# Choosing expert rows by float32 picks and an indexed fetch, and returning every pass's result through TensorE

## The chip, the core and the metric

The kernel runs on one core of one Trainium2 chip. The metric is device microseconds of one execution. The core has TensorE (PE; its weight loads are PEld), VectorE (DVE), ScalarE (ACT), GpSimd (POOL), a sync engine (SP) whose queue issues most transfers, and 16 DMA engines. [...]

## What is computed

One decoder layer on 512 tokens of width 1024: a mixer of mLSTM and sliding-window heads, a layer norm, a mixture of 32 experts, a second layer norm.

```python
x = layer_norm(ALPHA * x + hybrid_mixer(x, ...), ln1_w, ln1_b)
g_idx = argmax(x @ w_group_router + b_group_router)          # 4 groups
e_in = (x @ w_expert_router + b_expert_router)[8 experts of g_idx]
top_v, top_i = top_k(e_in, 2)
combine = one_hot(8 * g_idx + top_i) * softmax(top_v) * group_probability
for e in range(32):                                          # D_EXPERT = 256
    h = silu(x @ w_exp_gate[e]) * (x @ w_exp_up[e])
    out += combine[:, e] * (h @ w_exp_down[e])
x = layer_norm(ALPHA * x + out, ln2_w, ln2_b)
```

All tensors are float32. The weights of one expert are 3 MB.

## The kernel before

**Mixer.** Float32 products are made of a high and a low part in fp32r, three products each. The projection's weights come in eleven column groups; the first in three loads (`load_w`, `split_w`, `unit_att`). Small tables come on the GpSimd queue, among them the convolution's weights: `cw` in four transfers of 1,024 single float32 elements, `cb` in one.

**Router stage.** Tokens stand in four groups `c` of 128. For each the output projection (`out_mm`, `ml_late`) is summed in PSUM, then `norm_a` (statistics) and `norm_b` (application) give `x1[c]`; `route_t` transposes it, `route_m` multiplies by the router's weights, `route_d` finds two experts a token, `route_r` the rank of a token in its expert, `first_hot` the one-hot matrix of places. `NB` says for each half which engines apply the norm: V is two operations on DVE, the others go over ACT and POOL. `x1_hi` (ACT) and `x1_lo` (POOL) split `x1` into two fp32r parts. The order of PE, DVE, ACT and POOL is written out by hand in this stage.

**Expert passes.** Thirteen passes hold 128 places each, kinds `BBBCABABABBCC` (B: two experts, A: two, C: four). The first three passes have the experts 0 to 5 (their weights are fetched ahead); the others have experts by load, whose numbers `eid` come from `slots_a` and `slots_e`. A pass multiplies its rows `xs` by gate and up (`gu_part`), makes `h` (`pair_h`, `dn_t`) and multiplies by down (`dn_mm`). Rows come for two passes at a time: `first_pick` for passes 0 and 1, `pairs_x` for 2 to 11: 64 fp32r products of 128x256 with the one-hot of places (`pick`, L1014). Only pass 12 fetches rows of `x1` from DRAM (`xd`) by index, `fetch`, and transposes them. The results of passes 0 to 7 (`KEPT = 8`) are scaled and stored in DRAM (`y_store`, table `yd`); at passes 8 and 9 each token fetches its two rows (`y_fetch`, `y_add`). Passes 8 to 11 are added by TensorE: `add_back`, for each 128 tokens and half width two products of 128x512 (L1185) with the one-hot `back_hot` and one DVE addition.

**Transfers.** Expert weights come over SP's queue in pieces of 1 MB (a gate and an up piece of 512 KB each, or a down piece) into 16 ring slots (`ring0` 7, `ring1` 5, `ring2` 4) and two borrowed ones. A slot is loaded again after the products that read it (`release`, `prefetch`).

Of the kernel before, what the change touches and what calls it, by code (L numbers as in the profile page):

```python
# [80 lines left out]
def layer_kernel(ctx, tc, x, w_in, conv_w, conv_b, gate_bias, norm_w, sinks, w_out, ln1_w, ln1_b,  # L81
# [504 lines left out]

    def load_part(ts, e, i, js=None):
# [137 lines left out]
    x1, x1h, x1l, amh, mlm, pys = [], [], [], {}, {}, {}  # L725
# [151 lines left out]
    def norm_b(c, h):  # L877
        xc_ = x1[c]
        mv = n1[c][1]
        hs = slice(h * 512, (h + 1) * 512)  # L880
        xh_ = xc_[:, hs]
        if NB[c][h] == "V":
            V.scalar_tensor_tensor(xh_, xh_, mv[:, 0:1], l1w[:, hs], op0=OP.subtract, op1=OP.mult)
            V.scalar_tensor_tensor(xh_, xh_, mv[:, 2:3], l1b[:, hs], op0=OP.mult, op1=OP.add)
        else:
            if h == 0 or NB[c][0] == "V":
                G.tensor_scalar(mv[:, 3:4], mv[:, 2:3], mv[:, 0:1], -1.0, op0=OP.mult, op1=OP.mult)
            A.activation(xh_, xh_, AF.Identity, bias=mv[:, 3:4], scale=mv[:, 2:3])
            (V if NB[c][h] == "M" else G).tensor_mul(xh_, xh_, l1w[:, hs])
            G.tensor_add(xh_, xh_, l1b[:, hs])  # L890

    def x1_parts(c, halves):
        v = x1[c].rearrange("p (q j) -> p j q", j=8)
        if len(x1h) == c:
            for t, n in ((x1h, "x1h"), (x1l, "x1l")):
                t.append(slot(n, F32R)[:, :DM].rearrange("p (j q) -> p j q", j=8))
        for q in [slice(0, P)] if halves is None else [slice(64 * h, 64 * h + 64) for h in halves]:
            yield x1h[c][:, :, q], x1l[c][:, :, q], v[:, :, q]

    def x1_hi(c, halves=None):  # L900
        for hi, _, v in x1_parts(c, halves):
            A.activation(hi, v, AF.Copy)

    def x1_lo(c, halves=None, eng=G):
        for hi, lo, v in x1_parts(c, halves):
            eng.tensor_tensor(lo, v, hi, op=OP.subtract)
# [95 lines left out]
    def hot_tiles():  # L1002
        return slot("ohr", F32R)[:, :DM].rearrange("p (c s) -> p c s", c=NCH)

    def hot(o, c, col, n=2 * P):
        d, k = o[:, c, 0:n], iot[:, 0:n]
        V.tensor_scalar(d, k, col[:, 0:1], None, op0=OP.is_equal)
        yield
        V.scalar_tensor_tensor(d, k, col[:, 1:2], d.bitcast(F32), op0=OP.is_equal, op1=OP.add)
        yield  # L1010

    def pick(p_, j2, o, c, g, n=2):
        for s, w in enumerate((x1h, x1l)):
            TE.matmul(p_[:, j2, 0:P * n], w[c][:, 2 * g + j2], o[:, c, 0:P * n], start=c == 0 and s == 0 and j2 == 0,  # L1014
                      stop=c == NCH - 1 and s == 1 and j2 == 1)

    def pick_out(xs, p_, g, n=2, eng=None):
        d = xs[g // 2][:, 2 * (g % 2):2 * (g % 2) + 2, 0:P * n]
        if g % 2 and eng is None:
            V.tensor_copy(d, p_[:, :, 0:P * n])  # L1020
        else:
            A.copy(d, p_[:, :, 0:P * n])
# [4 lines left out]
    def hots(p, n=2 * P):  # L1027
        o, steps = hots_of(p, n)
        par(steps)
        return o  # L1030

    def hots_of(p, n=2 * P):
        ts = hot_tiles()

        def steps():
            t = W.tile([P, 8], F32, name="pcol")
            V.tensor_scalar(t, col, -float(P * p), None, op0=OP.add)
            yield
            for c in range(NCH):
                yield from hot(ts, c, t[:, 2 * c:2 * c + 2], n)  # L1040
        return ts, steps()

    def pairs_x(o, n):
        xs = xs_tiles()
        for g in range(4):
            p_ = bank("xp", tag="t").rearrange("p (j n) -> p j n", j=2)
            for j in range(2):
                for c in range(NCH):
                    pick(p_, j, o, c, g, n)
            pick_out(xs, p_, g, n)  # L1050
        return xs
# [21 lines left out]
    def ready(p):  # L1073
        return fetch(p) if p in GATHER else hots(p)

    def taken(p, t):
        return pairs_g(t) if p in GATHER else pairs_x(t, min(2, NP - p))

    oh0 = None

    def first_hot(c):
        nonlocal oh0
        if c == 0:
            oh0 = hot_tiles()
        return hot(oh0, c, cola[:, c])
# [62 lines left out]
    def y_store(py, p):  # L1148
        y = slot("y")[:, :DM]
        for u in range(2):  # L1150
            A.activation(y[:, 512 * u:512 * u + 512], py[u], AF.Copy, scale=cws[:, p:p + 1])  # L1151
        G.dma_start(yd[p * P:(p + 1) * P], y)  # L1152


    def y_fetch(c):
        ts = [slot("yg")[:, :DM] for _ in range(2)]
        for k, t in enumerate(ts):
            G.memset(t, 0.0)
            G.indirect_dma_start(out=t, out_offset=None, in_=yd[:, :],
                                 in_offset=bass.IndirectOffsetOnAxis(ap=yrow[:, 2 * c + k:2 * c + k + 1], axis=0),  # L1160
                                 bounds_check=KEPT * P - 1, oob_is_err=False)
# [38 lines left out]
    yrow = C.tile([P, 8], I32, name="yrow")  # L1200
# [98 lines left out]
    def slots_c():  # L1299
# [11 lines left out]
        V.tensor_copy(yrow, col)  # L1311
# [515 lines left out]
```

## Time and profile before

| | us |
|---|---|
| median of 3 runs | 522.66 (521.9 to 523.89) |
| profiled execution | 525.79 |
| its span, first to last instruction | 524.1 |
| mixer, from the start to the output projection | about 180 |
| router stage with the first picks | about 180 to 264 |
| thirteen passes and second norm | 264 to 524 |

The profiled execution is 3.1 us above the median. A view by stretches tells how busy each engine is in a stage and what the DMA engines moved; a view of waits tells what released an engine; the view in order of time gives the spacing of neighbouring instructions, which for pipelined products is their price (their own durations overlap).

### The profile page before, as it was taken

The numbers are of one execution on the slowest core, as the hardware profiler recorded it, in microseconds if no ns is written. First come the engines' busy times: TensorE is split into PE (matmuls) and PEld (weight loads), VectorE is DVE, ScalarE is ACT, GpSimd is POOL, SyncE is SP. The second block draws the span as 40 slices with busy tenths as digits, with TensorE's granted clock in tenths as the row PEclk, the third lists the DMA queues.
The fourth block names the chain that finished last, engine by engine and source line by source line (L and its number), as shares of the span: only waits on it lengthen the run. The fifth ranks groups of instructions, "written<-read, shape, count | busy, mean of one in ns | idle before, by whom it ended". The sixth has DMA issues, their size and how long they took to land. (4 is left out here: it accounts for less than half of the span.)

```text
span 524.1 us, 8258 instructions
## 1 busy us (share of the span) xinstructions
PE 477.0 (91%) x2960; PEld 321.5 (61%) x2960; DVE 281.5 (54%) x635; ACT 161.2 (31%) x349; POOL 155.8 (30%) x178
## 2 busy tenths in 40 slices
PE   5999799999999999979799999899899879899880
PEld 5999688879889987767644745263363443253320
DVE  3543697974288675688865303013032045576953
ACT  3552565785534422423221111111111010131310
POOL 3689805223210111636640000000011342300531
PEclk8899999999999999989799999989999879999996
DMA  7633112221974539095739999999999999999630
GB/s 229 218 108 121 56 39 92 69 82 43 361 281 108 178 118 283 35 372 184 304 129 349 401 348 410 384 418 420 390 410 406 403 422 413 421 419 420 259 161 21
DMA packets 36285, 134.71 MB, mean 257 GB/s; under 512 B 6734, under 2 KB 6750, under 8 KB 32912
## 3 DMA queue, kind: packets, MB, share of 16 engines
q1 hardware_dynamic: 33184, 126.04, 63.7%
q0 software_dynamic: 3056, 8.10, 4.2%
q8 instruction: 24, 0.39, 0.3%
q14 instruction: 21, 0.17, 0.1%
HBM read 127.11 MB, written 8.91 MB: 260 GB/s over the span
## 5 line engine op out<-in xcount | busy, mean ns | idle before, releaser
L1101 PE MATMUL pg<-we,xs 128*32 128x512 f32 (+1 forms) x608 | 102.8, 605 | 8.3 <-DMA we<-in_w_exp_up 8.3
L1101 PEld LDWEIGHTS pg<-we,xs 128*32 128x32 f32 (+1 forms) x608 | 27.6, 120 | 67.6 <-issue 62.8
L239 PE MATMUL pj<-wh,xh 128*128 128x256 f32 (+1 forms) x224 | 64.4, 289 | 3.9 <-ACT wh L190 3.9
L240 PE MATMUL pj<-wh,xl 128*128 128x256 f32 (+1 forms) x224 | 63.5, 285 | 0.3 <-DVE xl L191 0.3
L1014 PE MATMUL xp<-ohr,x1h 128*128 128x256 f32 x192 | 50.0, 299 | 5.5 <-DVE xs L1020 3.0
L244 PE MATMUL pj<-wl,xh 128*128 128x256 f32 x192 | 52.5, 280 | 0.0
L1134 PE MATMUL yo<-we,ht 128*32 128x512 f32 (+1 forms) x304 | 50.6, 620 | 0.5 <-DVE ht L1126 0.5
L1014 PE MATMUL xp<-ohr,x1l 128*128 128x256 f32 x192 | 48.7, 292 | 0.0
L239 PEld LDWEIGHTS pj<-wh,xh 128*128 128x128 f32 x224 | 43.2, 193 | 4.5 <-ACT wh L190 4.4
L1014 PEld LDWEIGHTS xp<-ohr,x1h 128*128 128x128 f32 x192 | 38.4, 200 | 10.6 <-issue 5.9
L240 PEld LDWEIGHTS pj<-wh,xl 128*128 128x128 f32 x224 | 43.2, 193 | 0.6 <-DVE xl L191 0.6
L1152 POOL DMA_DIRECT2D yd<-y x8 | 4.4, 553 | 128.5 <-ACT y L1151 128.5
L1126 DVE COPY ht<-ph 128x256 f32<-128x256 f32 x13 | 5.5, 423 | 65.1 <-PE ph L1124 65.1
L1116 ACT ACTIVATE hid<-pg 128x256 f32<-128x256 f32 x13 | 5.0, 385 | 109.9 <-PE pg L1101 109.9
L1014 PEld LDWEIGHTS xp<-ohr,x1l 128*128 128x128 f32 x192 | 38.3, 200 | 0.0
L244 PEld LDWEIGHTS pj<-wl,xh 128*128 128x128 f32 x192 | 35.6, 188 | 0.0
L191 DVE TENSOR_TENSOR wl<-wraw,wh 128x1024 fp32r<-128x1024 f32 x14 | 19.8, 1429 | 24.3 <-ACT wh L190 24.3
L1134 PEld LDWEIGHTS yo<-we,ht 128*32 128x32 f32 (+1 forms) x304 | 14.3, 123 | 28.6 <-issue 26.6
L190 ACT ACTIVATE wh<-wraw 128x1024 fp32r<-128x1024 f32 (+2 forms) x23 | 23.2, 1022 | 15.8 <-DMA wraw<-in_w_in 6.1
L194 PE MATMUL pj<-xh,wh 128*128 128x512 f32 x64 | 25.7, 402 | 0.0
L196 PE MATMUL pj<-xl,wh 128*128 128x512 f32 x64 | 25.5, 399 | 0.0
L199 POOL TENSOR_SCALAR lnmv<-lnmv 128x1 f32<-128x1 f32 x9 | 4.1, 451 | 72.1 <-DVE lnmv L1638 49.8
(355 smaller groups left out, 973.0 us busy)
## 6 DMA issues: line engine op xcount, KB each, us to landing
we<-in_w_exp_gate SPq DMA_DIRECT2D x64, 512.0 KB, 11.8
we<-in_w_exp_up SPq DMA_DIRECT2D x64, 512.0 KB, 8.9
we<-in_w_exp_down SPq DMA_DIRECT2D x26, 1024.0 KB, 14.3
wraw<-in_w_in SPq DMA_DIRECT2D x20, 512.0 KB, 4.6
we<-in_w_exp_down SPq DMA_DIRECT2D x12, 512.0 KB, 9.8
yd<-y POOLq DMA_DIRECT2D x8, 512.0 KB, 8.0
xc<-in_x_columns SPq DMA_DIRECT2D x4, 512.0 KB, 10.4
wo<-in_w_out SPq DMA_DIRECT2D x8, 256.0 KB, 4.1
```

Source lines behind the costliest of these rows:

```text
L190: A.activation(hi, src, AF.Copy)
L191: eng.tensor_tensor(lo, src, hi, op=OP.subtract)
L194: TE.matmul(o, lh, rh, start=start, stop=False)
L196: TE.matmul(o, lh, rl, start=False, stop=stop)
L239: TE.matmul(o, xh[j // 2][:, j % 2, cs], ws[i][j][0], start=j == 0, stop=False)
L240: TE.matmul(o, xl[j // 2][:, j % 2, cs], ws[i][j][0], start=False, stop=False)
L244: TE.matmul(o, xh[k // 2][:, k % 2, cs], ws[i][k][1], start=False, stop=k == 7)
L1014: TE.matmul(p_[:, j2, 0:P * n], w[c][:, 2 * g + j2], o[:, c, 0:P * n], start=c == 0 and s == 0 and j2 == 0, stop=c == NCH - 1 and s == 1 a ...
L1101: TE.matmul(pg[s:s + n], xs[k // 4][:, k % 4, P * b + s:P * b + s + n], ws[e][k // 4][:, :, k % 4], start=k == 0, stop=k == 7)
L1116: A.activation(h, pg[:, 0:256], AF.Silu)
L1126: V.tensor_copy(ht, ph)
L1134: TE.matmul(py[u][s:s + n], ht[:, j, s:s + n], wt[e][2][j][:, 512 * u:512 * u + 512], start=j == 0, stop=j == 1)
```

## The change

1. Passes 0 and 1 take their rows by float32 products of `x1` itself with the one-hot (128x128, no high and low part): 40 of these products (all of pass 0 and 8 of pass 1) before pass 0 begins, the other 24 behind its gate and up.
2. Passes 2 to 12 fetch rows by index from `xd` and transpose them (`pairs_g`).
3. All passes are returned by `add_back`; passes 0 and 1 together, four products a unit. `yd`, `y_store`, `y_fetch`, `y_add` go. The multiplication of `x1` by ALPHA moves from four POOL operations into the first addition.
4. The router stage has a new order; `norm_b` is on DVE for all halves; `x1_hi`, `x1_lo` go.
5. The table of rows (`slots_c`) is made ahead of pass 1's products instead of behind pass 0's down.
6. `conv_w`, `conv_b` and the router's weights are laid out by partition on the host, so `cw` is one transfer with 128 B in each partition; gate and up weights are laid out so that a partition holds rows k*128+p.

```diff
-    for j in range(4):
-        G.dma_start(cw[:, j], ap_of(conv_w, j * DM, [[1, P], [P, 8]]))
+    G.dma_start(cw, ap_of(conv_w, 0, [[32, P], [8, 4], [1, 8]]))
-    G.dma_start(cb, ap_of(conv_b, 0, [[1, P], [P, 8]]))
+    G.dma_start(cb, ap_of(conv_b, 0, [[8, P], [1, 8]]))
...
-    def first_pick(c, gs=range(4)):
+    def first_pick(c, ps=(0, 1)):
...
+        for b in ps:
+            for k in range(8):
+                TE.matmul(xp0[2 * b + k // 4][:, k % 4], x1[c][:, k * P:k * P + P], oh0[:, c, P * b:P * b + P],
+                          start=c == 0 and k % 4 == 0, stop=c == NCH - 1 and k % 4 == 3)
...
-    def add_back(o, y, cs=range(NCH)):
+    def add_back(oys, cs=range(NCH)):
+        mm = [(o, t) for o, y in oys for t in y]
...
-                for i, t in enumerate(y):
-                    TE.matmul(b, o[:, c * P:(c + 1) * P], t[:, us], start=i == 0, stop=i == 1)
-                V.tensor_add(x1[c][:, us], x1[c][:, us], b)
+                for i, (o, t) in enumerate(mm):
+                    TE.matmul(b, o[:, c * P:(c + 1) * P], t[:, us], start=i == 0, stop=i == len(mm) - 1)
+                if (c, u) in scaled:
+                    V.tensor_add(xu, xu, b)
+                else:
+                    scaled.add((c, u))
+                    V.scalar_tensor_tensor(xu, xu, ALPHA, b, op0=OP.mult, op1=OP.add)
...
-    for c in range(NCH):
-        G.tensor_scalar(x1[c], x1[c], ALPHA, None, op0=OP.mult)
...
             if p % 2:
-                xs = taken(p + 1, hn)
+                xs = pairs_g(hn)
                 if p + 3 < NP:
-                    hn = ready(p + 3)
+                    hn = fetch(p + 3)
```

GpSimd's queue from the first router norm to the last transfer of the passes. `lnmv` is the norm's small table, `l1w` and `l1b` its weight and bias, `x1l` the low part. Before, in three pieces:

```order
L200 TENSOR_TENSOR lnmv<-lnmv,mhalf 128x1
L887 TENSOR_SCALAR lnmv<-lnmv 128x1
L889 TENSOR_TENSOR x_2177<-x_2177,l1w 128x512
L890 TENSOR_TENSOR x_2177<-x_2177,l1b 128x512
...
L906 TENSOR_TENSOR x1l<-x_2183,x1h 128x1024
L906 TENSOR_TENSOR x1l<-x_2186,x1h 128x8x64 x2
L1522 TENSOR_SCALAR x_2177<-x_2177 128x1024
...
L1152 DMA yd<-y 128x1024 x7
L1158 MEMSET yg 128x1024 x2
L1152 DMA yd<-y 128x1024
L1158 MEMSET yg 128x1024
L1159 DMA yg<-yd,yrow 128x1024 x3
```

Now:

```order
L1279 MEMSET rsc 128x8x4
L194 TENSOR_SCALAR lnmv<-lnmv 128x1
L195 TENSOR_TENSOR lnmv<-lnmv,mhalf 128x1
...
L1000 DMA xg<-xd,row 128x1024 x11
L1449 TENSOR_TENSOR l2d<-l2w,pcol 16x512 x2
```

The wide operations on `x1` and all stores are gone from POOL; four pairs of one-column operations and eleven indexed fetches are left.

TensorE from the end of the router stage over passes 0 and 1 (`xp` picked or transposed rows, `pg` gate and up, `ph` the transposed `h`, `yo` down, `lg` and `xcum` small router sums, `slot` the table of rows). Before:

```order
L1238 MATMUL lg<-rsc 1x32
L1101 MATMUL pg<-we,xs 64x512 x4
L1244 MATMUL xcum<-triu,sn 128x32
...
L1101 MATMUL pg<-we,xs 64x512 x20
L1124 MATMUL ph<-ident,hid 128x128 x2
...
L1303 MATMUL slot<-ohbk,ohrk 64x116 x8
L1134 MATMUL yo<-we,ht 64x512 x8
L1014 MATMUL xp<-ohr,x1h 128x256
L1014 MATMUL xp<-ohr,x1l 128x256
```

Now:

```order
L1032 MATMUL xp<-ohr,x_2181 128x128 x8
L1044 MATMUL pg<-we,xs 64x512 x4
L1169 MATMUL lg<-rsc 1x32
L1175 MATMUL xcum<-triu,sn 128x32
...
L1044 MATMUL pg<-we,xs 64x512 x8
L1032 MATMUL xp<-ohr,x_2175 128x128 x8
L1032 MATMUL xp<-ohr,x_2178 128x128 x8
L1032 MATMUL xp<-ohr,x_2181 128x128 x8
L1234 MATMUL slot<-ohbk,ohrk 64x116 x8
L1044 MATMUL pg<-we,xs 64x512 x12
...
L1012 MATMUL xp<-ident,xg 128x128 x16
```

Pass 1's picks and the table of rows stand between the gate-up products of pass 0 and of pass 1; the next rows are 16 transposes instead of 64 picks.

TensorE at pass 5, a B pass (`cb` the add-back product, `yh` and `yl` the two parts of a result). Before:

```order
L1134 MATMUL yo<-we,ht 32x512 x16
L1101 MATMUL pg<-we,xs 64x512 x12
L1124 MATMUL ph<-ident,hid 128x128 x2
L1101 MATMUL pg<-we,xs 64x512 x4
L1014 MATMUL xp<-ohr,x1h 128x256
L1014 MATMUL xp<-ohr,x1l 128x256
```

Now:

```order
L1077 MATMUL yo<-we,ht 32x512 x16
L1044 MATMUL pg<-we,xs 64x512 x4
L1113 MATMUL cb<-yh,oh_3455 128x512
L1113 MATMUL cb<-yl,oh_3455 128x512
...
L1044 MATMUL pg<-we,xs 64x512 x4
L1067 MATMUL ph<-ident,hid 128x128 x2
...
L1012 MATMUL xp<-ident,xg 128x128 x16
```

Each quarter of a pass's gate and up is followed by four add-back products of the pass before the last.

## Rows read from the trace of the kernel before

**Rows 1.** Page of the profiled execution, parts 1 and 2: busy time, share of the span and instructions of each engine; and the busy share of the 16 DMA engines in 40 equal slices of 13.1 us, in tenths.

```profile
PE 477.0 (91%) x2960; PEld 321.5 (61%) x2960; DVE 281.5 (54%) x635; ACT 161.2 (31%) x349; POOL 155.8 (30%) x178
DMA  7633112221974539095739999999999999999630
```

**Rows 2.** Stretches of the span: length, then busy us (instructions) of PE, PEld, DVE, ACT, POOL, then the granted TensorE clock, the DMA share and GB/s. The router stage with the first picks, the first two passes, and three stretches of the later passes.

```profile
178.00:265.00 87.00, 76.85 (x418) 63.51 (x418) 64.93 (x152) 31.31 (x51) 37.24 (x31) 0.94 0.58 208
265.00:300.00 35.00, 35.00 (x202) 18.91 (x200) 17.64 (x55) 4.70 (x9) 4.24 (x4) 1.00 0.86 320
340.00:380.00 40.00, 37.85 (x238) 17.41 (x239) 7.08 (x17) 5.08 (x9) 1.07 (x2) 0.96 1.02 409
380.00:420.00 40.00, 36.82 (x250) 19.20 (x249) 8.89 (x25) 5.29 (x9) 8.98 (x10) 0.96 1.02 407
420.00:460.00 40.00, 34.60 (x181) 14.52 (x180) 21.92 (x34) 4.11 (x8) 13.42 (x11) 0.91 1.02 419
```

**Rows 3.** Waits of TensorE from 262 us to the end: line that waited, releaser, us in total, times, longest.

```profile
PE pg L1101 <- DMA we<-in_w_exp_up: 8.3, 5, 2.3
PE xp L1014 <- DVE xs L1020: 3.0, 1, 3.0
```

**Rows 4.** Start of the kernel in order of time, TensorE and then ScalarE: start us, us, operation [idle before it, releaser]. The second third of the first weight group.

```profile
11.38 0.59 PE L239 MATMUL pj<-wh,xh 128*128 128x264 f32 x1 [3.62 <-ACT wh L190]
...
10.46 0.86 ACT L190 ACTIVATE wh<-wraw 128x792 fp32r<-128x792 f32 x1 [3.88 <-DMA wraw<-in_w_in]
```

**Rows 5.** Start of the kernel on the GpSimd queue, in order of time, and the row of the DMA issues for the same loads (count, KB each, median us from issue to landing).

```profile
3.34 2.69 POOL L694 DMA_DIRECT2D cw<-in_conv_w  x3
13.21 0.90 POOL L694 DMA_DIRECT2D cw<-in_conv_w  x1 [7.17 <-issue]
...
cw<-in_conv_w POOLq DMA_DIRECT2D x4, 4.0 KB, 9.6
```

**Rows 6.** Two stretches of 2 us at the start; columns as in rows 2.

```profile
8.00:10.00 2.00, 0.00 (x0) 0.00 (x0) 0.00 (x0) 0.00 (x0) 0.00 (x0) 0.94 1.02 327
10.00:12.00 2.00, 0.62 (x3) 0.62 (x4) 0.64 (x1) 1.54 (x3) 0.00 (x0) 0.50 1.05 239
```

**Rows 7.** Waits of TensorE in the router stage, 196 to 265 us; columns as in rows 3.

```profile
PE lg L986 <- DVE ohs L957: 5.9, 4, 2.4
PE xp L1014 <- DVE ohr L1009: 2.5, 3, 1.6
```

**Rows 8.** Two stretches of the router stage; columns as in rows 2.

```profile
228.00:240.00 12.00, 9.26 (x37) 7.19 (x36) 9.41 (x28) 0.98 (x2) 2.62 (x5) 0.86 0.66 270
248.00:256.00 8.00, 5.74 (x29) 5.48 (x29) 6.45 (x25) 3.31 (x10) 3.81 (x3) 0.57 1.01 410
```

**Rows 9.** VectorE in the router stage in order of time: one operation of the first 128 tokens, and the same one of the second.

```profile
222.58 2.27 DVE L994 SCALAR_TENSOR_TENSOR cola<-idf,rank 128x2 f32<-128x2 f32 x1
232.56 0.16 DVE L994 SCALAR_TENSOR_TENSOR cola<-idf,rank 128x2 f32<-128x2 f32 x1
```

**Rows 10.** GpSimd in order of time: the low half of the first 128 tokens, and the four multiplications by ALPHA.

```profile
221.81 3.02 POOL L906 TENSOR_TENSOR x1l<-x,x1h 128x1024 fp32r<-128x1024 f32 x1
256.94 11.07 POOL L1522 TENSOR_SCALAR x<-x 128x1024 f32<-128x1024 f32 x4 [0.85 <-DMA xd<-x]
```

**Rows 11.** TensorE in order of time (start us, us, operation): two groups of float32 products of 128x129 (two records each product), two neighbouring picks of 128x256, eight transposes of 128x128, two neighbouring add-back products of 128x512.

```profile
152.16 0.61 PE L536 MATMUL ni<-va,st 128*128 128x129 f32 x4
152.61 0.61 PE L541 MATMUL nc<-csa,qk 128*128 128x129 f32 x4
...
240.50 0.28 PE L1014 MATMUL xp<-ohr,x1l 128*128 128x256 f32 x1
240.61 0.28 PE L1014 MATMUL xp<-ohr,x1h 128*128 128x256 f32 x1
...
151.29 1.04 PE L409 MATMUL pt<-ident,pr 128*128 128x128 f32 x8
...
440.60 0.39 PE L1185 MATMUL cb<-yl,oh 128*128 128x512 f32 x1
440.82 0.39 PE L1185 MATMUL cb<-yh,oh 128*128 128x512 f32 x1
```

**Rows 12.** TensorE in order of time: the last product of the output projection, the first of pass 0, of pass 4, of pass 10 and of pass 11.

```profile
240.14 0.40 PE L196 MATMUL py<-wol,mls 128*128 128x512 f32 x1
...
264.28 1.94 PE L1101 MATMUL pg<-we,xs 128*64 128x512 f32 x8
...
323.01 5.36 PE L1101 MATMUL pg<-we,xs 128*32 128x512 f32 x48
...
432.02 1.94 PE L1101 MATMUL pg<-we,xs 128*64 128x512 f32 x8
...
447.94 1.92 PE L1101 MATMUL pg<-we,xs 128*32 128x512 f32 x16
```

**Rows 13.** The sync engine's queue: the first load of an expert that the routing chose; and the GpSimd queue's packets, MB and share of 16 engines' span.

```profile
268.59 0.36 SPq L591 DMA_DIRECT2D we<-in_w_exp_gate  x1
...
q0 software_dynamic: 3056, 8.10, 4.2%
```

**Rows 14.** VectorE over the whole span: second half of a layer-norm application, count, busy us, mean ns, idle before it.

```profile
L884 DVE SCALAR_TENSOR_TENSOR x<-x,lnmv,l1b 128x512 f32<-128x512 f32 x4 | 3.0, 752 | 2.4 <-POOL lnmv L200 2.3
```

More of the change, by code (lines that the diff above doesn't have):

```diff
@@ L881, in norm_b @@
         xh_ = xc_[:, hs]
[L882 to L906, printed above, removed]
+        V.scalar_tensor_tensor(xh_, xh_, mv[:, 0:1], l1w[:, hs], op0=OP.subtract, op1=OP.mult)
+        V.scalar_tensor_tensor(xh_, xh_, mv[:, 2:3], l1b[:, hs], op0=OP.mult, op1=OP.add)
     xts = {}
@@ L1002, in hot_tiles, with hot, hots @@
     def hot_tiles():
-        return slot("ohr", F32R)[:, :DM].rearrange("p (c s) -> p c s", c=NCH)
-    def hot(o, c, col, n=2 * P):
-        d, k = o[:, c, 0:n], iot[:, 0:n]
+        return slot("ohr")[:, :DM].rearrange("p (c s) -> p c s", c=NCH)
+    def hot(o, c, col, lo=0, hi=2 * P):
+        d, k = o[:, c, lo:hi], iot[:, lo:hi]
         V.tensor_scalar(d, k, col[:, 0:1], None, op0=OP.is_equal)
         yield
-        V.scalar_tensor_tensor(d, k, col[:, 1:2], d.bitcast(F32), op0=OP.is_equal, op1=OP.add)
+        V.scalar_tensor_tensor(d, k, col[:, 1:2], d, op0=OP.is_equal, op1=OP.add)
         yield
[L1012 to L1022, printed above, removed]
     def xs_tiles():
         return [slot("xs")[:, :DM].rearrange("p (j n) -> p j n", j=4) for _ in range(2)]
[L1027 to L1032, printed above, removed]
-        ts = hot_tiles()
[L1035 to L1038, printed above, removed]
-            for c in range(NCH):
[L1040 to L1051, printed above, removed]
+    def hots(p):
+        ts = hot_tiles()
+        t = W.tile([P, 8], F32, name="pcol")
+        V.tensor_scalar(t, col, -float(P * p), None, op0=OP.add)
+        for c in range(NCH):
+            par(hot(ts, c, t[:, 2 * c:2 * c + 2], 0, P))
+        return ts
     def fetch(p):
@@ new lines, in layer_kernel @@
+        norm_a(1, (1,))
+        norm_b(0, 1)
+        out_mm(2, 0, (0,), (0, 1))
+        route_t(0, (0,))
+        out_mm(2, 0, (0,), (2, 3))
+        route_t(0, (1,))
+        norm_b(1, 0)
+        norm_b(1, 1)
+        out_mm(3, 1, (0,), (0, 1))
+        route_m(0)
+        norm_a(2, (0,))
+        rd(0, 19)
+        route_t(1)
+        out_mm(3, 1, (0,), (2, 3))
+        rr(0, 9)
+        par(first_hot(0))
+        route_m(1)
+        rd(1, 19)
+        out_mm(3, 1, (1,), (0, 1))
+        out_mm(3, 1, (1,), (2, 3))
@@ L1503, in layer_kernel @@
     prefetch(N2)
-    for c in range(NCH):
-        if c not in kept:
-            keep(c)
-    hn, steps = hots_of(2)
+    keep(2)
+    keep(3)
+    hts = []
     with tc.manual_schedule(engines={ENG.PE}):
-        par(route_w())
         sb = slots_b(px)
         some(sb, 2)
+        first_pick(1, (1,))
         h = pair_h(pgs[0])
-        hts = []
+        par(route_w())
+        first_pick(2, (1,))
+        par(sb)
+        first_pick(3, (1,))
+        first_out(1)
+        slots_c()
+        hn = fetch(2)
         pgs.append(pass_gu(xs, 1, 1, lambda: hts.append(dn_t(h))))
-        par(chain(sb, steps))
+        slots_d()
         h = pair_h(pgs[1])
@@ L1581, in back, with later @@
         return back_hot(slot("oh2", F32R)[:, 0:T], toks(p))
-    def later(o, y):
-        return [lambda c=c: add_back(o, y, (c,)) for c in range(NCH)]
-    parts = ()
+    def later(oys):
+        return [lambda c=c: add_back(oys, (c,)) for c in range(NCH)]
     with tc.manual_schedule(engines={ENG.PE, ENG.DVE}):
+        parts = later([(back(p), y_split(pys[p], cws[:, p:p + 1], *y_slots())) for p in range(2)])
         for p in range(2, NP - 1):
@@ L1758, in layer_kernel @@
         split(yh, yl, held_y)
[L1759 removed]
+        add_back([(back_hot(slot("oh2", F32R)[:, 0:T], toks(NP - 1)), (yh, yl))])
         for c in range(NCH):
@@ L1785, in rope_tables, with by_partition @@
             np.ascontiguousarray(np.concatenate([-s, s], 1)))
+def by_partition(w):
+    v = np.asarray(w)
+    if v.shape[1] == DM and v.ndim == 3:
+        return v.reshape(DM // P, P, -1).transpose(1, 0, 2)
+    return v.reshape(-1, DM // P, P).transpose(2, 0, 1)
 def by_groups(w):
```

215 lines of the change are left out of this document (67 added, 148 removed).

## The prediction

> **What bounds the kernel now.** I read the page first, then the stretches, then the waits and single instructions where a stretch is not full. TensorE is busy 91% of the span, and the DMA engines are full from slice 24 on [rows 1], so each stage has to be asked which of the two it waits for.
>
> At the start it is neither: TensorE stands idle 3.62 us for the second third of the first weights, whose raw tile comes late from the DMA [rows 4]. Nearly nothing else happens there; the DMA engines are full all the same, and what they move falls from 327 to 239 GB/s [rows 6], while GpSimd's queue has the convolution's weights under way, which take 9.6 us to land [rows 5].
>
> In the router stage, 178 to 265 us, TensorE works 76.85 of 87 us and the DMA engines stand at 0.58 [rows 2], so neither is full. The waits name a chain between TensorE and VectorE: 5.9 us for the split one-hot sums (L986 on L957), 2.5 us for the one-hot of places [rows 7]. [...] Part of VectorE's own slowness comes from GpSimd: the same small operation takes 2.27 us while GpSimd writes the low half of `x1`, and 0.16 us ten microseconds later [rows 9, 10].
>
> In the passes the DMA engines are full (share 1.02, 407 to 419 GB/s from 340 to 460 us) and TensorE nearly so [rows 2]; after 262 us it waits 8.3 us for weights and 3.0 us for rows, the latter behind the additions of fetched results on VectorE [rows 3]. From pass 4 to pass 10 the kernel takes 109.0 us, 36.3 for two passes [rows 12]. That is the pace of the DMA engines; TensorE alone would be somewhat quicker, as is worked out below.
>
> **Start.** Five loads of single float32 elements (4 x 1,024 and 1,024) become two loads with 128 and 32 bytes per partition. If they are what holds the weights up, most of the 3.62 us goes, and the clock, which is 0.50 behind that wait [rows 4, 6], comes back earlier: if that level lasts some 4 us, twice the stretch shown, it costs 2 us of work (an estimate). Bounds: nothing (the weights are late on their own account) and 3.6 + 1.9 = 5.5 us. I take 3.5, since the rate fell by 27% at a full share [rows 6], which a plain load of large pieces doesn't do here.
> [...]
>
> **Router stage.** What can be won: the two waits, 5.9 + 2.5 = 8.4 us [rows 7], and the time lost to the lower clock, 12 x 0.14 + 8 x 0.43 = 5.1 us [rows 8], together 13.5. `x1_lo` and the wide halves of the norm leave GpSimd, so the stretching in [rows 9] loses its cause, and the new order puts output products of tokens 2 and 3 between the router's steps of tokens 0 and 1. What it costs:
> - Picks ahead of pass 0: 64 products of 128x256 at 0.11 to 0.12 us (240.50 to 240.61) are 7.7 us; now 40 float32 products. Two of 128x129 with a new left side each take 0.45 us (152.16 to 152.61), so 0.225 each and 9.0 us [rows 11]: +1.3.
> - All norm halves on VectorE: 2 operations of 0.752 us each [rows 14] for four more halves, 6.0 us. VectorE is busy 64.93 of 87 us [rows 2] and the first pairs lie under output products; the last pair stands on the path, +1.5. Without that cover it would be +6.
> - Some waiting stays, since the chain from the last norm to pass 0 is as serial as before (24.1 us from the last output product to the first of pass 0 [rows 12], picks in it): +1.2.
> Sum −13.5 + 4.0 = −9.5. Bounds: −3 (half of the 13.5 comes back) and −13 (no cost shows).
>
> **Passes, TensorE.** Five pairs lose 64 picks (7.7 us) for 16 transposes (8 take 1.04 us [rows 11], so 2.1): −28. Eight passes more are returned by 16 products of 0.22 us [rows 11]: +28, and one VectorE addition each, in place of one for fetched rows. The 24 picks behind pass 0: 24 x 0.225, +5.4. Pass 10 already had its share of `add_back` and no picks: 15.9 us to pass 11 [rows 12]. Two such passes with 16 transposes are 33.9 us, under the present 36.3, so TensorE alone doesn't hold the passes to today's pace.
>
> **Passes, DMA.** Eight stores of 0.52 MB (4.19 MB) go, and the fetches of these results: all results would be 4.19 MB, 8 of 13 passes about 2.6. The software queue's total of 8.10 MB [rows 13] leaves room for both. Ten fetches of 0.52 MB come: 5.24. Net −1.55 MB, at 409 GB/s [rows 2] −3.8 us. Against it, pass 1's weights are let go later after pass 0's start: its picks (5.4) and the table of rows stand ahead of it, some 7 us. The DMA engines have 14% to spare from 265 to 300 us [rows 2], 4.9 us, so about 2.1 are lost. The numbers of routed experts come behind a quarter or two of pass 0, but their first load starts 4.3 us after pass 0 anyhow [rows 12, 13]. Sum −1.7, I take −1.5. Bounds: −6.8 (the 3.0 us of [rows 3] goes too, the slots cost nothing) and +5.5 (fetched rows run no better than the stores, late picks wholly on the path). ALPHA's four multiplications (11.07 us of GpSimd [rows 10]) go at no gain: they lie under pass 0 and nobody on the path waits for them. The last passes' `add_back` and the second norm are as before, so an earlier last weight moves the end one to one.
>
> Sum: −3.5 − 9.5 − 1.5 = −14.5. The profiled execution of 525.79 becomes 511.3. It is 3.1 above the median of 522.66, which becomes 508.2: **508 us**. By the bounds alone −25 to +2.5.
>
> **Rivals.** 0.5% is 2.6 us, about what a measurement of this kernel can tell.
> - The start gains nothing (0.13): the weights are late by their own 327 GB/s. [...]
> - The stage gains half (0.14): VectorE with all norm halves (64.93 + 6.0 of a shorter stage) sets the pace instead of the waits. 513 us.
> - Slots late (0.12): pass 1's weights and the first fetches, which need the table and rows stored in `xd`, hold the DMA stream back by what the stage won. For it: the stream is full from 300 on and only its start counts. Against: the share of 0.86 before that. 508 + 9.5, 518 us.
> - Both bounds give way together (0.09): stage −13, passes −6.8, start −3.5, −23.3 in all: 499 us.
> - The other side (0.11): with products of 0.22 us between quarters of weights that arrive late, TensorE falls to its lower clock level in the passes. Each pair's 32 added products then take 7.0 us more, 33.9 becomes 40.9, 4.6 above today's 36.3; over four pairs 18 us, without the 1.5 won there: 525.8 − 13 + 18 = 531, in the median 528. It decides as soon as a pair costs TensorE more than 36.3. For it: clocks of 0.91 to 0.96 with only 8.3 us of waits [rows 2, 3]. Against: add-back products give TensorE work of its own while weights come, and pass 10 with them took 15.9.
> [...]
>
> **How the numbers follow.** The forecast itself has 0.38 (503 to 515), other mishaps 0.03. From 498 to 520 us all but the other side and the tails are held, somewhat over 8 in 10. Faster by over 0.5%: 0.38 + 0.13 + 0.14 + 0.09 and half of the third rival, 0.80; within 0.5% the other half and a part of the rest, 0.08; slower 0.12.
>
> **What would show it.** Start: TensorE's wait for the second third falls from 3.62 to about 1 us, with no clock of 0.50 behind it. Stage: the waits on `ohs` and on `ohr` fall below 2 us in sum, the small operation at L994 takes 0.2 us for the first tokens too, pass 0 starts near 251 and the first routed load near 256. Passes: the DMA share stays 1.0, a pair takes 34 to 36 us, the software queue moves 6 to 7 MB, GpSimd is nearly idle. The prediction is wrong if the clock in the passes is under 0.9, if a new wait stands before pass 0, or if TensorE waits for fetched rows.

## The result

The changed kernel takes 507.01 us (median of 4 runs, 506.32 to 509.89) against 522.28 us of the kernel before on the same chip. The medians' quotient is 0.971; a program sometimes runs in a slower state, so the ratios here and below are estimated from the fast runs alone, here 0.974, interval 0.970 to 0.978. The forecast was 508, range 498 to 520. The sum came out right, though its terms did not: the start gave nothing, and other terms made up for it.

The page of the profiled execution (507.21 us, span 505.5): busy time of each engine, and in tenths over 40 slices TensorE's granted clock (a share of its full speed) and the DMA engines' share.

```profile
PE 477.5 (94%) x2912; PEld 313.2 (62%) x2912; DVE 301.4 (60%) x680; ACT 149.9 (30%) x340; POOL 107.7 (21%) x142
...
PEclk8999989999999999999999999999999999999996
DMA  8523212220892654509988999999999999999740
```

TensorE is busy as long as before, 477.5 us for 477.0 [rows 1], in a span 18.6 us shorter: the difference is time in which it stood idle, 47 us before and 28 now.

Stretches, columns as in [rows 2]: the router stage, the first two passes, two stretches of the later ones.

```profile
178.00:255.00 77.00, 75.45 (x445) 61.95 (x446) 57.00 (x170) 19.20 (x40) 7.16 (x13) 1.00 0.64 229
255.00:290.00 35.00, 34.73 (x196) 19.20 (x194) 16.79 (x39) 5.65 (x10) 5.85 (x6) 1.00 0.91 321
330.00:370.00 40.00, 39.76 (x224) 15.90 (x222) 20.78 (x36) 5.38 (x9) 1.87 (x2) 1.00 1.02 412
```

TensorE works 75.45 of 77 us in the stage (76.85 of 87 before) at a clock of 1.00, and GpSimd is busy 7.16 us there in place of 37.24 (some 8 of these were ALPHA's multiplications [rows 10]). In the passes TensorE is now as full as the DMA engines: 39.76 of 40 us at 1.00, where it was 37.85 of 40 at 0.96 with the same DMA share [rows 2].

Waits of TensorE, first in the stage, then from 250 us to the end:

```profile
PE rt L890 <- ACT x1T L891: 0.7, 1, 0.7
PE lg L1137 <- DVE rkt L962: 0.3, 1, 0.3
...
PE pg L1044 <- DMA we<-in_w_exp_up: 2.2, 1, 2.2
PE ph L1067 <- DVE hid L1060: 1.7, 1, 1.7
```

Both waits of [rows 7] are gone, 0.7 us is the longest that took their place. After them the 8.3 us for weights and the 3.0 for rows of [rows 3] are down to one wait of 2.2.

TensorE in order of time: its restart after the first weights, first and last product of the output projection, first products of passes 0, 10 and 11.

```profile
10.20 0.59 PE L234 MATMUL pj<-wh,xh 128*128 128x264 f32 x1 [2.23 <-ACT wh L185]
...
179.47 0.50 PE L189 MATMUL py<-woh,ams 128*128 128x512 f32 x1
...
233.59 0.39 PE L191 MATMUL py<-wol,mls 128*128 128x512 f32 x1
...
251.41 1.94 PE L1044 MATMUL pg<-we,xs 128*64 128x512 f32 x8
...
414.95 1.94 PE L1044 MATMUL pg<-we,xs 128*64 128x512 f32 x8
...
430.76 1.49 PE L1044 MATMUL pg<-we,xs 128*32 128x512 f32 x12
```

The same first product of the output projection in the kernel before:

```profile
179.74 0.50 PE L194 MATMUL py<-woh,ams 128*128 128x512 f32 x1
```

Between these marks and those of [rows 12] the two profiled executions differ as follows: start and mixer −0.3 us (179.74 to 179.47), router stage −12.6 (from 84.5 to 71.9), pass 0 to pass 11 −4.3 (from 183.7 to 179.4), from there to the end of the span −1.4. The execution of before that was profiled is 3.5 us above its median, so these add up to 18.6 where the medians differ by 15.3. One pair of executions doesn't fix the size of a term: the stage in particular differs by some us between executions of one kernel (last section).

### The profile page after: what moved, and what is told of

The parts are those of the page before. It is cut to its first block, busy times and chain, and to the rows that moved or that the text cites. A ratio compares the mean times of both kernels' runs of the same rounds, so it can differ in the third digit from the quotient of the medians.

```text
span 505.5 us, 8207 instructions
## 1 busy us (share of the span) xinstructions
PE 477.5 (94%) x2912; PEld 313.2 (62%) x2912; DVE 301.4 (60%) x680; ACT 149.9 (30%) x340; POOL 107.7 (21%) x142
## 3 DMA queue, kind: packets, MB, share of 16 engines
q0 software_dynamic: 2096, 6.54, 3.7%
## 5 line engine op out<-in xcount | busy, mean ns | idle before, releaser
L1044 PE MATMUL pg<-we,xs 128*32 128x512 f32 (+1 forms) x608 | 100.5, 599 | 2.2 <-DMA we<-in_w_exp_up 2.2
L1115 DVE TENSOR_TENSOR x<-x,cb 128x512 f32<-128x512 f32 x80 | 51.3, 682 | 23.7 <-PE cb L1113 23.3
L239 PE MATMUL pj<-wl,xh 128*128 128x256 f32 x192 | 53.3, 283 | 0.0
L1077 PE MATMUL yo<-we,ht 128*32 128x512 f32 (+1 forms) x304 | 48.8, 597 | 0.5 <-DVE ht L1069 0.5
L1113 PE MATMUL cb<-yh,oh 128*128 128x512 f32 x96 | 42.6, 444 | 1.8 <-DVE x L1115 1.3
L1113 PE MATMUL cb<-yl,oh 128*128 128x512 f32 x96 | 38.0, 396 | 0.4 <-DVE yl L1088 0.4
L1113 PEld LDWEIGHTS cb<-yh,oh 128*128 128x128 f32 x96 | 18.1, 188 | 32.6 <-issue 22.5
L1000 POOL DMA_INDIRECT xg<-xd,row x11 | 10.5, 957 | 128.8 <-PE cb L1113 64.3
L239 PEld LDWEIGHTS pj<-wl,xh 128*128 128x128 f32 x192 | 36.3, 192 | 0.0
L186 DVE TENSOR_TENSOR wl<-wraw,wh 128x1024 fp32r<-128x1024 f32 x14 | 21.4, 1544 | 23.3 <-ACT wh L185 17.8
L1088 DVE SCALAR_TENSOR_TENSOR yl<-yo,cws,yh 128x512 fp32r<-128x512 f32 x24 | 17.7, 749 | 18.4 <-ACT yh L1087 17.4
L1087 ACT ACTIVATE yh<-yo,cws 128x512 fp32r<-128x512 f32 x24 | 16.4, 688 | 37.0 <-PE yo L1077 36.7
```

Of the source, the lines that this page charges most:

```text
L186: eng.tensor_tensor(lo, src, hi, op=OP.subtract)
L239: TE.matmul(o, xh[k // 2][:, k % 2, cs], ws[i][k][1], start=False, stop=k == 7)
L1044: TE.matmul(pg[s:s + n], xs[k // 4][:, k % 4, P * b + s:P * b + s + n], ws[e][k // 4][:, :, k % 4], start=k == 0, stop=k == 7)
L1077: TE.matmul(py[u][s:s + n], ht[:, j, s:s + n], wt[e][2][j][:, 512 * u:512 * u + 512], start=j == 0, stop=j == 1)
L1088: V.scalar_tensor_tensor(yl[:, us], py[u], cs, yh[:, us], op0=OP.mult, op1=OP.subtract)
L1115: V.tensor_add(xu, xu, b)
```

## What the experiments show

Ratios are to the kernel before on the same chip, 521.8, 522.7 and 523.5 us in the three groups of runs.

**The start.** The convolution's layout alone, put into the kernel before:

```diff
-    for j in range(4):
-        G.dma_start(cw[:, j], ap_of(conv_w, j * DM, [[1, P], [P, 8]]))
+    G.dma_start(cw, ap_of(conv_w, 0, [[32, P], [8, 4], [1, 8]]))
-    G.dma_start(cb, ap_of(conv_b, 0, [[1, P], [P, 8]]))
+    G.dma_start(cb, ap_of(conv_b, 0, [[8, P], [1, 8]]))
```

> The kernel before with the convolution's weights and bias laid out by partition (part 6 alone, two transfers in place of five). In the traces TensorE restarts after the first weights at 11.38 us before and at 10.20 after the whole change, but the first product of the output projection starts at 179.74 and 179.47. Theory 1, the start is worth what its wait shows and something later in the mixer ate it by chance: restart near 10.2, the ACT step at 26.6 near 24.4, output projection near 177.5, time 522.3 - 2.2 = 520.1. Theory 2, the mixer has a later point that doesn't come earlier: restart near 10.2, output projection at 179.4 to 179.8, time 522 to 522.6.

521.19 us, ratio 0.999 (0.995 to 1.002): no difference, and a gain of 3.5 us (0.993) is outside the interval. Its restart and its first product of the output projection:

```profile
10.36 0.59 PE L239 MATMUL pj<-wh,xh 128*128 128x264 f32 x1 [2.45 <-ACT wh L190]
...
178.56 0.50 PE L194 MATMUL py<-woh,ams 128*128 128x512 f32 x1
```

And the reverse, the changed kernel with the old five transfers (the same diff read upwards):

> The kernel after with the old five transfers of single elements for the convolution. Theory 1: restart of TensorE near 11.4, output projection 2 us later than 179.47, time 507.0 + 2 = 509. Theory 2: restart near 11.4, output projection within 0.5 of 179.5, time 507.0 to 507.5.

505.27 us, 0.971 (0.963 to 0.979) of before, not slower than the changed kernel. With single elements TensorE restarts there at

```profile
10.33 0.59 PE L234 MATMUL pj<-wh,xh 128*128 128x264 f32 x1 [2.05 <-ACT wh L185]
```

and in another kernel with the old transfers (the norm experiment below) earlier still:

```profile
9.44 0.39 PE L239 MATMUL pj<-wh,xh 128*128 128x264 f32 x1 [1.48 <-ACT wh L190]
```

So the wait for the second third of the first weights does not hang on these loads. In the traces of the kernels with single elements it ends at 11.38, 10.27, 9.44 and 10.33 us, in the ten with the new layout at 9.12 to 11.48, on the mean 10.4 and 10.6: it wanders by two microseconds from one execution to the next, with both layouts. The 3.62 us of [rows 4] were one draw. What the changed kernel's own trace had won by 63 us (2.3 us, the first score product at 62.99 for 65.27) it lost again by 179 us, part of it to the clock from 60 to 72 us (last section). The new layouts of the router's and of the experts' weights were not tried alone.

**What held the router stage.** The kernel before in its old order, with the first picks made from `x1` itself, so that nobody needs the low part in the stage:

```diff
-                pick(xp0[g], j, oh0, c, g)
+                TE.matmul(xp0[g][:, j, 0:2 * P], v[:, 2 * g + j], oh0[:, c, 0:2 * P], ...)
...
-        x1_lo(0)
...
+    for c in range(NCH):       # behind the gate and up of pass 0
+        x1_hi(c)
+        x1_lo(c)
```

> The kernel before, old order, with the first picks by float32 products of x1 itself (32 of 128x256) and the low and high parts of x1 made only behind the first products of pass 0, so GpSimd writes no low part in the router stage. Theory, GpSimd's wide operations stretch VectorE's and so make the waits: waits on ohs and ohr in the stage fall from 8.4 to 3 us or less, the small operation at L994 takes 0.2 us in the first tokens too; picks cost 32 x 0.43 = 13.8 in place of 7.7 us; pass 0 starts near 264.3 - 5.4 + 6 = 265 and the time is within 3 us of 522. Rival, the order makes the waits: they stay near 8 and pass 0 starts near 270.

528.33 us, 1.012 (1.006 to 1.017). Waits of TensorE in the stage, and behind it:

```profile
PE lg L986 <- DVE ohs L957: 1.1, 1, 1.1
...
PE ph L1126 <- DVE hid L1119: 8.5, 2, 6.8
```

VectorE at the place of [rows 9]:

```profile
222.22 0.16 DVE L994 SCALAR_TENSOR_TENSOR cola<-idf,rank 128x2 f32<-128x2 f32 x1
...
223.08 0.48 DVE L1009 SCALAR_TENSOR_TENSOR ohr<-iot,cola,ohr 128x256 f32<-128x256 f32 x1
```

The theory's mechanism is there: 0.16 us where it was 2.27, 1.1 us of waits in place of 8.4, and the stage takes 80.2 us (179.35 to 259.52) in place of 84.5 although the picks take 17.6 us (0.55 each, where 0.43 was expected), part of it at a lower clock (0.87 from 240 to 248 us, 0.92 from 248 to 256), in place of 7.7. With the changed kernel's 9.3 us of picks in their place it would be 71.9, which is what the changed kernel's stage takes: by this estimate the new order and the norm on VectorE add nothing of their own. It is no more than an estimate, since the longer picks may also have covered waits. The total was forecast wrong (within 3 us of 522): the parts of `x1` and ALPHA's multiplications now keep GpSimd at work from 261 to 285 us, while VectorE makes the table of rows and `h` of pass 0, and TensorE waits 8.5 us for `h`, where it waited 1.7 before. That GpSimd's wide work does the harm here too, where VectorE stands on the path, is my reading of this.

The reverse, GpSimd's wide work put into the changed kernel, one subtraction a token group, read by nobody:

```diff
+    def low(c):
+        G.tensor_tensor(spare, x1[c]..., l1w..., op=OP.subtract)
...
+        low(0)
         rr(0, 9)
```

> The kernel after with four subtractions of 128x1024 on GpSimd put back into the router stage, one a token group, right before the rank steps on VectorE; nobody reads what they write. Theory, GpSimd's wide operations stretch VectorE's and so make the waits: the small operation at the rank step takes 2 us or more beside them, TensorE waits 4 to 8 us more in the stage, pass 0 starts at 255.5 to 259.5 in place of 251.4 and the time is 510 to 515. Rival, the new order made the gain and stands the stretching: pass 0 within 1.5 us of 251.4, time 506 to 508.5.

520.37 us, 0.994 (0.990 to 0.997) of before: most of the gain is gone, and with this work on GpSimd the stage is as long in the new order as it was in the old. GpSimd's first such operation starts as soon as its tokens are normalised, not at the rank step. It, and VectorE in order of time beside it:

```profile
213.12 3.10 POOL L1320 TENSOR_TENSOR spare<-x,l1w 128x1024 f32<-128x1024 f32 x1
```

```profile
211.97 0.75 DVE L878 SCALAR_TENSOR_TENSOR x<-x,lnmv,l1b 128x512 f32<-128x512 f32 x1
212.64 0.75 DVE L877 SCALAR_TENSOR_TENSOR x<-x,lnmv,l1w 128x512 f32<-128x512 f32 x1
213.49 3.28 DVE L878 SCALAR_TENSOR_TENSOR x<-x,lnmv,l1b 128x512 f32<-128x512 f32 x1
216.69 0.74 DVE L877 SCALAR_TENSOR_TENSOR x<-x,lnmv,l1w 128x512 f32<-128x512 f32 x1
```

An operation of 0.75 us takes 3.28 us: it ends half a microsecond after GpSimd's (213.12 + 3.10 = 216.22). It isn't slowed in proportion; its end follows GpSimd's. So does that of the operation of [rows 9] in the kernel before: 222.58 + 2.27 = 224.85, with GpSimd's of [rows 10] ending at 221.81 + 3.02 = 224.83. Not all of VectorE's work is held: beside GpSimd's second subtraction (218.35 to 221.36) the statistics of 128x512 (L867, one input) take their usual 0.69 us, and then a small operation on 128x4 with two inputs (L915, usually 0.16) takes 1.46 and ends at 221.39. The number of inputs alone doesn't decide: in the kernel before, just ahead of the operation of [rows 9] and beside the same work of GpSimd, one with two inputs (`lg` is a sum in PSUM) and one with one take 0.22 us each, with the other tokens 0.22 and 0.18 to 0.22,

```profile
222.07 0.22 DVE L990 TENSOR_TENSOR rkt<-rsc,lg 128x64 f32<-128x64 f32 x1 [0.20 <-PE lg L986]
222.33 0.22 DVE L992 TENSOR_REDUCE rank<-rkt 128x2 f32<-128x64 f32 x1
```

while beside ALPHA's multiplications [rows 10] one with one input and a column of scalars (`cola`) takes 1.20 us, and 0.34 to 0.35 with the three other groups of tokens:

```profile
258.71 1.20 DVE L1007 TENSOR_SCALAR ohr<-iot,cola 128x256 fp32r<-128x256 f32 x1
```

What makes VectorE wait for GpSimd, no run here separates. What follows on TensorE (the profile names no releaser for the first wait; it ends at 246.79, when the second stretched half of a norm does), waits and two stretches with the clock (last column but two):

```profile
PE rt L890 <- issue: 3.1, 1, 3.1
PE lg L958 <- DVE ohs L929: 2.9, 2, 2.3
```

```profile
220.00:228.00 8.00, 5.71 (x26) 4.86 (x25) 5.81 (x26) 1.30 (x4) 1.37 (x1) 0.74 0.00 0
248.00:256.00 8.00, 7.43 (x36) 6.88 (x36) 6.63 (x30) 1.65 (x10) 2.86 (x1) 0.50 1.02 397
```

Four operations of 3 us make the stage 85.7 us (178.58 to 264.31) in place of 71.9: about 6 us of waits, and most of the rest is the clock behind them, down to 0.50. I had expected half of that, having counted the stretched operations and not the clock behind the waits; and the operation at the rank step, which I had named, was not touched (0.16 us).

The norm alone, in the kernel before:

```diff
-NB = ('VA', 'MA', 'VA', 'VV')
+NB = ('VV', 'VV', 'VV', 'VV')
```

> The kernel before, old order, with all halves of the norm's application on VectorE (four more). Theory, GpSimd's wide norm operations are slow and stretch VectorE: pass 0 starts 1 to 3 us earlier than 264.28, time 519 to 521. Rival C of the prediction, VectorE's 6.0 us more bound the stage: pass 0 starts 2 to 4 us later, time 524 to 526.

(Rival C is the prediction's second, "the stage gains half".) 522.79 us, 1.003 (0.999 to 1.007): no difference, so neither expectation held. Pass 0 starts at 264.54; the stage takes 85.8 us, where the two executions with the old norm took 84.5 and 82.2. Of TensorE's waits in it three stand out:

```profile
PE rt L918 <- DVE gms L938: 3.5, 1, 3.5
PE lg L986 <- DVE ohs L957: 3.3, 3, 2.4
PE xp L1014 <- DVE ohr L1009: 2.1, 2, 1.3
```

In the old order the norm on VectorE takes 2.6 us from the wait on `ohs` and makes a new one of 3.5 us for the first tokens' maximum (`gms`). VectorE's added work is not free in the old stage. In the new one it is covered; whether the low parts' absence or the new order makes room for it, no run here separates.

**What sets the pace of the passes.** The changed kernel without the return of passes 0 to 7 (their products and additions are left out):

```diff
-                parts = later([(back(p - 1), y_split(...))])
+                parts = later([(back(p - 1), y)]) if p - 1 >= 8 else ()
```

> The kernel after without the return of passes 0 to 7 (their results are still scaled, but 128 products and the VectorE additions are left out). Theory DMA, the transfers set the pace of the passes: from pass 0 to pass 10 still 160 to 163.5 us, TensorE waits for weights in place of the products, time 503 to 507. Theory TensorE, which is busy 39.76 of 40 us there: 128 x 0.22 = 28 us of products go, from pass 0 to pass 10 150 us or less, time under 497.

505.96 us, 0.967 (0.961 to 0.973): 28 us of products less, and 1 us of time by the medians, 3 to 4 by the ratios. TensorE's wait for weights over the passes, and the stretch shown above for the changed kernel:

```profile
PE pg L1044 <- DMA we<-in_w_exp_up: 22.4, 15, 3.6
...
330.00:370.00 40.00, 31.51 (x184) 10.49 (x182) 6.42 (x11) 4.69 (x8) 1.87 (x2) 1.00 1.02 414
```

TensorE has 8 us more to spare there, and the transfers run on as before, at 414 GB/s for 412. Pass 0 to pass 10 is 8 us shorter (155.3, a little under what I expected of the transfers), and 6 of these are given back before the last pass. The transfers set the end. The other side of it, 0.52 MB more at each of ten passes:

```diff
             prefetch(99)
+            SP.dma_start(yd[(p - 2) * P:(p - 1) * P], x2[0:P])
```

> The kernel after with a transfer of 0.52 MB from DRAM to DRAM added at each of the passes 2 to 11, that nobody waits for. Theory DMA: 5.24 MB more at 412 GB/s, 12.7 us, pass 0 to pass 10 in 174 us or more, time 517 to 521. Theory TensorE: the DMA engines have room, pass 0 to pass 10 within 3 us of 163.5, time under 510.5.

520.26 us, 0.997 (0.994 to 1.001) of before: 13.3 more than the changed kernel by the medians, 12 by the ratios, so 2.3 to 2.5 us a MB; at 412 GB/s it would be 2.4. By pass 10 only 3.6 of it shows (167.2 us), so what was expected there did not come; the ring of slots lends the rest and the last passes pay. The transfers bind, but not alone: in the changed kernel TensorE waits only 2.2 us for weights in all its passes, and it is busy 39.76 of 40 us, so by my estimate fewer bytes would soon meet TensorE's own pace. No run here tries that.

**The early table.** The table of rows and the first fetch moved back behind pass 0's down:

```diff
-        slots_c()
-        hn = fetch(2)
         pgs.append(pass_gu(xs, 1, 1, ...))
...
         ht = dn_t(h)
+        slots_c()
+        hn = fetch(2)
         pys.append(pass_dn(ht, 1))
```

> The kernel after with the table of rows and the first fetch behind pass 0's down, as the table was before, so the rows of pass 2 are asked for some 20 us later. Theory, the early table is needed by the fetch: a new wait of TensorE for the fetched rows of 3 to 8 us at pass 2, given back in part since the transfers go on meanwhile: time 507 to 513. Rival, not needed: no such wait, time 506 to 508.

(Pass 1's down also moved ahead of the transposes of pass 2's rows.) 521.40 us, 0.996 (0.992 to 0.999): nearly the whole gain, and 8 us beyond what was expected. The first fetch on GpSimd's queue, in this kernel and in the changed one, and TensorE's wait for its rows:

```profile
284.20 1.15 POOL L1000 DMA_INDIRECT xg<-xd,row  x1 [46.35 <-DVE row L1241]
```

```profile
269.32 1.15 POOL L1000 DMA_INDIRECT xg<-xd,row  x1 [31.81 <-DMA we<-in_w_exp_gate]
```

```profile
PE xp L1012 <- DMA xg<-xd,row: 8.6, 2, 6.4
```

The rows are 15 us later (3 of them its later pass 0); TensorE waits 8.6, and pass 2 starts 45.4 us after pass 0 in place of 33.4. The weights that wait for slots go out later, the next gate piece at 315.4 us in place of 298.5, and the stream of weights runs dry before it fills again:

```profile
290.00:330.00 40.00, 33.41 (x174) 16.06 (x176) 13.73 (x25) 5.43 (x10) 3.14 (x4) 0.84 0.74 275
```

From 290 to 330 us 275 GB/s instead of 409: a third of 40 us is 13. From pass 0 to the end this execution takes 11.2 us more than the changed kernel's; another 3.1 of its 14.6 are the lower clock in the stage (last section). This is the third rival's mechanism, and what the change avoids by its part 5. It is also the price that the fetch brings: the old picks needed only the places, not the table.

All 64 picks ahead of pass 0, so that the last 24 no longer stand behind its gate and up:

```diff
         par(first_hot(3, P, 2 * P))
+        first_pick(1, (1,)); first_pick(2, (1,)); first_pick(3, (1,)); first_out(1)
         pgs = [bank("pg")]
```

> The kernel after with all 64 picks ahead of pass 0 (24 behind its gate and up before). Pass 0 starts at 257 in place of 251.4. Theory, the late picks cover VectorE's making of the table (256.6 to 265): without them TensorE waits 3 to 6 us for the table of rows, all is 5 to 6 us later, time 511 to 514. Rival, the 5.6 us only change place: the table comes at 268 as now, pass 2 starts within 1.5 us of 284.8, time 506 to 508.5.

517.94 us, 0.990 (0.983 to 0.996); the theory's sign, at twice its size. The last 40 of TensorE's picks (two records each) and the first product of pass 0, and its new wait:

```profile
251.44 9.20 PE L1032 MATMUL xp<-ohr,x 128*128 128x128 f32 x80
260.56 1.94 PE L1044 MATMUL pg<-we,xs 128*64 128x512 f32 x8
```

```profile
PE slot L1234 <- DVE ohbk L1227: 4.9, 1, 4.9
```

The picks cost 5.4 us ahead of pass 0. Behind it they are spared, but the wait for the table, 4.9 us, takes their place (the late picks cover VectorE's 8 us of work on it), and the clock behind this wait is lower, 0.72 from 274 to 284 us: pass 2 starts 35.5 us after pass 0 in place of 33.4. This execution had the lower clock in the stage besides (last section), some 3 us, which with 5.4, 2.1 and a mixer 0.7 longer makes its 11.

ALPHA's multiplications back on GpSimd:

```diff
+    for c in range(NCH):
+        G.tensor_scalar(x1[c], x1[c], ALPHA, None, op0=OP.mult)
```

> The kernel after with the four multiplications of x1 by ALPHA put back on GpSimd (and taken out of the first addition). As the prediction has it, they lie beside pass 0 and nobody waits: time 506 to 508.5. Rival, after the four subtractions on GpSimd cost 13 us: here they stand ahead of the first fetch in GpSimd's queue and beside VectorE's steps for the table, the fetch is issued at 274 to 280 in place of 269.3, TensorE waits 3 to 8 us for the rows of pass 2, time 510 to 517.

509.64 us, 0.974 (0.967 to 0.980) of before, the changed kernel's own ratio: no difference that can be measured, though the time itself lies between the two ranges. But the fetch does stand behind them, 3.5 us later than in the changed kernel, of which 2.1 are its later pass 0:

```profile
264.39 8.26 POOL L1429 TENSOR_SCALAR x<-x 128x1024 f32<-128x1024 f32 x3 [9.68 <-PE xp L1032]
272.83 1.13 POOL L1000 DMA_INDIRECT xg<-xd,row  x1 [0.18 <-issue]
```

TensorE waits 0.9 us for the rows and 0.9 for the table. So the rival's mechanism is there, at a size too small to tell.

**More slots.** Since the transfers set the end, one and two more borrowed slots (`LENT`, 2 before):

```diff
-LENT = 2
+LENT = 4
-    loads[4:10] = loads[6:9] + loads[4:6] + loads[9:10]
+    loads[4:12] = loads[6:9] + loads[4:6] + loads[10:12] + loads[9:10]
```

> The kernel after with one more borrowed slot for a down piece (three for two), so one routed piece can be asked for before pass 0 frees a slot. Theory, the transfers set the end: 1.05 MB at 412 GB/s, up to 2.5 us earlier, time 504 to 506. Rival, the working tiles that lend it are then short and give a new wait: time 507 to 511.

> The kernel after with two more borrowed slots for down pieces (four for two). Theory as with three: up to 5 us earlier, time 502 to 505.5. Rival, too few working tiles: a new wait of TensorE in passes 0 to 2, time 508 or more.

507.97 us, 0.971 (0.964 to 0.978), and 510.17, 0.975 (0.968 to 0.981): no gain that can be measured. The DMA engines from 250 to 270 us with four, and in the changed kernel:

```profile
250.00:270.00 20.00, 20.00 (x142) 13.85 (x142) 13.08 (x50) 4.01 (x6) 0.00 (x0) 1.00 0.64 208
```

```profile
250.00:270.00 20.00, 20.00 (x136) 13.38 (x136) 11.76 (x41) 4.01 (x6) 0.68 (x1) 1.00 0.91 329
```

The static weights are all there earlier, but the routed ones can't be asked for before their numbers are known (the first is at 256.2 us, 255.9 without the slots), so a slot more only leaves a hole of 0.64 ahead of them. With four TensorE also waits 2.1 us for the first fetched rows, so the rival held in part. The trace with three had the lower clock in the stage, some 3 us, so a small gain could hide in it.

## Why the prediction was right, by its own steps

- **Start, −3.5: wrong, it is nothing.** The step that failed read one execution's 3.62 us as the price of the single-element loads, because both stood in the same stretch. With either layout, in either kernel, the restart falls within the same two microseconds, and the first of the rivals held (0.13, the start gains nothing). The mean restarts, 10.4 us with single elements and 10.6 with the new layout, show no gain from the layout.
- **Router stage, −9.5: the mechanism right, the size about right.** The waits vanish, the operation of [rows 9] takes 0.16 us, the 40 picks 9.3 us by their spacing (I had 9.0). In two executions the old stage takes 84.5 and 82.2 us, the new one 71.9 to 72.1 without a clock drop in it (five traces) and 75.0 with one (three): −10.3 between the means, −7.2 to −12.6 from single traces. Of the 2.7 us that I put against the gain for the last norm pair and for waits that stay, 1.0 shows as waits. The second rival, VectorE with all norm halves as the pace, didn't come: VectorE is busy 57.00 of 77 us.
- **Passes, −1.5: the sign right, the size 1 to 3 us short.** The software queue moved 6.54 MB (the row below) for 8.10, −1.56 for my −1.55, and a MB is worth 2.3 to 2.5 us: −3.6 to −3.9. The 2.1 us that I set against it, for pass 1's slots, don't show in the sum; that TensorE has hardly a wait left of its own that would hold a slot is my reading, no run tests it. Pass 0 to pass 11 falls by 2.2 to 4.3 us, against three executions with the old passes, and pass 10 to 11 takes 15.8 us as forecast (15.9). The gain isn't spread evenly: pass 0 to 4 takes 3.9 us more than before (62.6 for 58.7), pass 4 to 10 8.1 less (100.9 for 109.0). So the old 36.3 us of a pair were not the bare pace of the transfers, as the prediction read them; TensorE's waits and its lower clock were in them.

```profile
q0 software_dynamic: 2096, 6.54, 3.7%
```

- **TensorE's side:** two passes take 33.6 us on the mean from pass 4 to 10 (314.05 to 414.95); 33.9 was forecast, 36.3 is the old pace. The other side's condition, over 36.3, wasn't met, and the clock stayed at 1.00 (from 290 to 450 us). The 7.0 us of that side are 32 products at double price. At the start of the kernel before a clock of 0.50 does cost about that: products of 128x264 (L239, L240) stand 0.22 us apart there from 12 to 13 us, and 0.12 apart from 17 to 18 us at 1.00.
- **ALPHA at no gain, the tail unchanged:** ALPHA put back has the changed kernel's ratio, which is known to some 3 us; the tail from pass 11 on takes 74.6 to 76.2 us in the four traces with the old passes, 74.7 and 72.5 in the changed kernel and the one with the old convolution loads, so it is some 1 to 2 us shorter at most.
- **The third rival** (slots and fetches late) is real, as the table's experiment shows, and would have cost nearly the whole gain. In the changed kernel TensorE waits for no fetched row. In its sum the prediction counted the early table only as a cost to pass 1's slots; it is what the gain hangs on.

So −14.5 was made of a term of −3.5 that isn't there, of a stage about 1 us short, of passes 1 to 3 us short and of a tail about 1 us short. That the sum is within 1 us of the measured −15.3 is luck: the misses cancel.

## What to carry to other kernels

A wait in one profiled execution is a sample: before its removal is priced, see in a second execution whether it is as long (here 3.62 us, and 1.48 to 2.40 in three others with the same loads). Look at what GpSimd does while VectorE stands on the path, since beside a subtraction of 3.0 to 3.1 us an operation there took 2.1 to 2.5 us more here (2.27 for 0.16, 3.28 for 0.75), and behind TensorE's waits the clock was 0.57 and 0.50 in these two kernels. Where transfers are full to the end, the work worth moving is what starts the stream and what feeds it without a hole, here the table that the first fetch needs (late, it left 275 GB/s for 409 from 290 to 330 us).

## What the hardware showed

The same instructions of the stage ran in two ways. From 236 to 240 us TensorE is busy 3.3 of 4 us in both of these kernels, with the same order up to pass 0; then the granted clock differs, in the changed kernel and in the one with the late table:

```profile
236.00:240.00 4.00, 3.32 (x28) 2.92 (x27) 3.83 (x6) 1.14 (x2) 1.43 (x2) 1.00 1.02 415
244.00:248.00 4.00, 3.69 (x42) 3.63 (x41) 2.92 (x21) 1.30 (x9) 0.00 (x0) 1.00 1.03 367
```

```profile
236.00:240.00 4.00, 3.33 (x28) 2.92 (x28) 3.83 (x7) 0.80 (x2) 1.66 (x2) 1.00 1.03 417
244.00:248.00 4.00, 4.00 (x20) 4.00 (x20) 2.93 (x20) 1.08 (x7) 0.00 (x0) 0.50 1.01 372
```

With the clock at 0.50 in this stretch (0.94 from 248 to 252 us) the 32 records of picks take 5.57 us in place of 3.82, and the stage 75.0 us in place of 71.9. The traces with this stage code and no more work in it divide into 71.9 to 72.1 (four besides the changed kernel's own, with the old convolution loads, without the returns, with more transfers, and with four slots borrowed) and 75.0 (three: the late table, ALPHA on GpSimd, three slots); the one with all 64 picks ahead had the lower clock too. The changed kernel has a like stretch in the mixer, a clock of 0.86 from 60 to 72 us behind a wait of 2.4 us, where the kernel before had 1.00 behind one of 2.3. In these nine executions the two stretches go together: the five without a drop in the stage all have 0.86 in the mixer, and the four with one in the stage all have 1.00 there. What decides which of the two comes stays open.
